# Six static tiles in a max-pool-and-subtract kernel, and subtracts without a wait for the slot's last stores

## The chip, the cores and the metric

The kernel runs on one core of one Trainium2 chip. The time is the device time of one execution in microseconds (us). It was 628.31 us, the median of 3 executions (628.23 to 628.38), before the change. "Span" is the time between the first and last thing in the profile; it is some 2 us shorter than the device time.

## The reference

```python
def reference(x):                                  # x: 8 x 64 x 256 x 256, float32
    x_r = x.reshape(B, C, oH, 8, oW, 8)
    pooled = x_r.max(axis=(3, 5))                  # maximum of each 8 x 8 window
    upsampled = np.repeat(np.repeat(pooled, 8, axis=2), 8, axis=3)
    return (x - upsampled).astype(np.float32)
```

134.2 MB come in and 134.2 MB go out. There is no matrix product.

## The kernel before

The work is cut into 32 tiles of 128 partitions. A full tile has 4 rows of 2048 numbers a partition: 32 KB a partition, 4096 KB in all. The loads are issued from SyncE's queue, the stores from ScalarE's; VectorE (DVE) takes the maximum of the windows in one reduce and subtracts row by row, in place. Tiles come from a pool of six that rotate: when tile i + 6 is asked for, the pool gives it the slot (the memory) of tile i and the framework adds what waits it thinks are needed. A wait goes by a semaphore, a counter that a transfer or an engine raises and that an instruction waits on.

```python
TILES = [([2, 2], [2, 2])] + [([4], [4])] * 30 + [([4], [2, 1, 1])]    # rows per load, rows per store
BUFS = 6
    data = ctx.enter_context(tc.tile_pool(name="data", bufs=BUFS))
    small = ctx.enter_context(tc.tile_pool(name="small", bufs=BUFS))

    def pool_and_subtract(dat, tops, R):
        # ... wins is dat by windows; one tensor_reduce (max) of R rows into tops
        for r in range(R):
            nc.vector.tensor_tensor(out=wins[:, r], in0=wins[:, r],
                in1=tops[:, r].unsqueeze(1).unsqueeze(3).to_broadcast([P, pH, oW, pW]),
                op=mybir.AluOpType.subtract)

    for loads, stores in TILES:
        dat = data.tile([P, size * ROW], F32, name="dat")
        pooled = small.tile([P, size * oW], F32, name="pooled")
        # ... cut: addresses
        for R in loads:
            nc.sync.dma_start(out=dat[:, part], in_=src[:, part])
        for R in stores:
            pool_and_subtract(dat[:, part], pooled[:, lo * oW : (lo + R) * oW], R)
            nc.scalar.dma_start(out=dst[:, part], in_=dat[:, part])
```

Of the kernel before, what the change touches and what calls it, by code (L numbers as in the profile page):

```python
# [1 line left out]

# [4 lines left out]

F32 = mybir.dt.float32
ROW = 2048

TILES = [([2, 2], [2, 2])] + [([4], [4])] * 30 + [([4], [2, 1, 1])]
BUFS = 6


@with_exitstack
def kernel(
    ctx: ExitStack,
    tc: tile.TileContext,
    x: bass.AP,
    out: bass.AP,  # L20
):
    nc = tc.nc
    P = nc.NUM_PARTITIONS
    B, C, H, W = x.shape
    pH = pW = 8
    oW = W // pW

    x_rows = x.rearrange("b c (oh ph) w -> (b c oh) (ph w)", ph=pH)
    out_rows = out.rearrange("b c (oh ph) w -> (b c oh) (ph w)", ph=pH)
    assert sum(sum(loads) for loads, _ in TILES) * P == x_rows.shape[0]  # L30
    size = max(sum(loads) for loads, _ in TILES)

    data = ctx.enter_context(tc.tile_pool(name="data", bufs=BUFS))
    small = ctx.enter_context(tc.tile_pool(name="small", bufs=BUFS))

    def pool_and_subtract(dat, tops, R):

        wins = dat.rearrange("p (r ph ow pw) -> p r ph ow pw", r=R, ph=pH, ow=oW)
        tops = tops.rearrange("p (r ow) -> p r ow", r=R)
        if R == 1:  # L40
            nc.vector.tensor_reduce(  # L41
                out=tops[:, 0],
                in_=wins[:, 0].rearrange("p ph ow pw -> p ow ph pw"),
                axis=mybir.AxisListType.XY,
                op=mybir.AluOpType.max,
            )
        else:
            nc.vector.tensor_reduce(  # L48
                out=tops,
                in_=wins.rearrange("p r ph ow pw -> p r ow ph pw"),  # L50
                axis=mybir.AxisListType.XY,
                op=mybir.AluOpType.max,
            )
        for r in range(R):
            nc.vector.tensor_tensor(  # L55
                out=wins[:, r],
                in0=wins[:, r],
                in1=tops[:, r].unsqueeze(1).unsqueeze(3).to_broadcast([P, pH, oW, pW]),
                op=mybir.AluOpType.subtract,
            )  # L60

    ctx.enter_context(tc.manual_schedule())
    at = 0
    for loads, stores in TILES:
        dat = data.tile([P, size * ROW], F32, name="dat")
        pooled = small.tile([P, size * oW], F32, name="pooled")

        rows = sum(loads)
        src = x_rows[at : at + P * rows].rearrange("(p r) d -> p (r d)", r=rows)
        dst = out_rows[at : at + P * rows].rearrange("(p r) d -> p (r d)", r=rows)  # L70
        at += P * rows
        lo = 0
        for R in loads:
            part = slice(lo * ROW, (lo + R) * ROW)
            nc.sync.dma_start(out=dat[:, part], in_=src[:, part])
            lo += R
        lo = 0
        for R in stores:
            part = slice(lo * ROW, (lo + R) * ROW)
            pool_and_subtract(dat[:, part], pooled[:, lo * oW : (lo + R) * oW], R)  # L80
            nc.scalar.dma_start(out=dst[:, part], in_=dat[:, part])
            lo += R


# [1 line left out]
_INS = ['x']  # L86
_OUTS = [((8, 64, 256, 256), 'float32')]


# [23 lines left out]
```

## Time and profile before

| | before |
|---|---|
| device time, median | 628.31 us |
| VectorE busy | 562.6 us, 90% of the span |
| VectorE idle, waiting for a load | 52.1 us |
| mean rate of the 16 DMA engines | 429 GB/s, 423 to 435 in the flat part |
| instructions in the profile | 364 |

The prediction below shows the lines behind this table. The busy engine is not the limit: VectorE waits for loads, while the DMA row shows its engines busy in every slice. This is the page's list of DMA queues (queue and kind: packets, MB, share of 16 engines), with the packet total ahead of it:

```profile
DMA packets 9794, 268.46 MB, mean 429 GB/s; under 512 B 1088, under 2 KB 1088, under 8 KB 1088
## 3 DMA queue, kind: packets, MB, share of 16 engines
q1 hardware_dynamic: 4752, 134.22, 49.9%
q10 hardware_dynamic: 5040, 134.22, 49.7%
q14 instruction: 2, 0.02, 0.0%
```

q1 and q10 are the loads and the stores. q14 carries instructions to the core (below, a fetch): two packets of 8192 bytes in the whole run, a share that prints as 0.0%.

### The profile page before, as it was taken

The numbers are of one execution on the slowest core, as the hardware profiler recorded it, in microseconds if no ns is written. First come the engines' busy times: TensorE is split into PE (matmuls) and PEld (weight loads), VectorE is DVE, ScalarE is ACT, GpSimd is POOL, SyncE is SP. The second block draws the span as 40 slices with busy tenths as digits, with TensorE's granted clock in tenths as the row PEclk, the third lists the DMA queues.
The fourth block names the chain that finished last, engine by engine and source line by source line (L and its number), as shares of the span: only waits on it lengthen the run. The fifth ranks groups of instructions, "written<-read, shape, count | busy, mean of one in ns | idle before, by whom it ended". The sixth has DMA issues, their size and how long they took to land.

```text
span 626.5 us, 364 instructions
## 1 busy us (share of the span) xinstructions
DVE 562.6 (90%) x163; POOL 0.2 (0%) x4
## 2 busy tenths in 40 slices
DVE  4999999988898888988889888899888898888983
POOL 0000000000000000000000000000000000000000
DMA  8999999999999999999999999999999999999997
GB/s 368 402 447 424 435 435 435 435 435 435 435 435 432 433 427 431 427 429 435 435 435 433 435 435 435 435 435 435 433 435 433 425 433 433 423 435 435 435 434 337
DMA packets 9794, 268.46 MB, mean 429 GB/s; under 512 B 1088, under 2 KB 1088, under 8 KB 1088
## 3 DMA queue, kind: packets, MB, share of 16 engines
q1 hardware_dynamic: 4752, 134.22, 49.9%
q10 hardware_dynamic: 5040, 134.22, 49.7%
q14 instruction: 2, 0.02, 0.0%
HBM read 134.22 MB, written 134.22 MB: 428 GB/s over the span
## 4 chain that ended last, share of the span: by engine, by line
DVE 90%; another core or an unknown queue 7%; DMA 1%; issue 0%
DVE dat L55 45%; DVE pooled L48 44%; DMA dat<-in_x_dram 1%; DVE pooled L41 1%
## 5 line engine op out<-in xcount | busy, mean ns | idle before, releaser
L48 DVE TENSOR_REDUCE pooled<-dat 128x128 f32<-128x8192 f32 (+1 forms) x33 | 273.8, 8297 | 52.1 <-DMA dat<-in_x_dram 52.1
L55 DVE TENSOR_TENSOR dat<-dat,pooled 128x2048 f32<-128x2048 f32 x128 | 285.0, 2287 | 1.2
L41 DVE TENSOR_REDUCE pooled<-dat 128x32 f32<-128x2048 f32 x2 | 4.6, 2278 | 0.0
L97 POOL MEMSET const-bfloat16-1.0<- 128x1 bf16 x1 | 0.1, 101 | 0.0
L97 POOL MEMSET const-uint8-127<- 128x1 uint8 x1 | 0.1, 101 | 0.0
L97 POOL MEMSET const-float32-0.0<- 128x1 f32 x1 | 0.1, 98 | 0.2 <-issue 0.2
L97 POOL MEMSET const-float32-1.0<- 128x1 f32 x1 | 0.1, 98 | 0.0
## 6 DMA issues: line engine op xcount, KB each, us to landing
dat<-in_x_dram SPq DMA_DIRECT2D x31, 4096.0 KB, 62.4
out_dram<-dat ACTq DMA_DIRECT2D x30, 4096.0 KB, 36.0
out_dram<-dat ACTq DMA_DIRECT2D x3, 2048.0 KB, 19.8
dat<-in_x_dram SPq DMA_DIRECT2D x2, 2048.0 KB, 9.5
out_dram<-dat ACTq DMA_DIRECT2D x2, 1024.0 KB, 10.4
```

What stands on the lines that cost most here:

```text
L41: nc.vector.tensor_reduce(out=tops[:, 0], in_=wins[:, 0].rearrange("p ph ow pw -> p ow ph pw"), axis=mybir.AxisListType.XY, op=mybir.AluOp ...
L48: nc.vector.tensor_reduce(out=tops, in_=wins.rearrange("p r ph ow pw -> p r ow ph pw"), axis=mybir.AxisListType.XY, op=mybir.AluOpType.max,)
L55: nc.vector.tensor_tensor(out=wins[:, r], in0=wins[:, r], in1=tops[:, r].unsqueeze(1).unsqueeze(3).to_broadcast([P, pH, oW, pW]), op=mybir ...
L97: nc = _bacc.Bacc("TRN2", target_bir_lowering=False, num_devices=1)
```

## The change

The intent: a subtract should not have to wait for the stores that last read its slot, because the load of the tile has already waited for them. Six tiles are allocated once and used in turn, and each subtract is declared independent of those stores.

```diff
-    data = ctx.enter_context(tc.tile_pool(name="data", bufs=BUFS))
-    small = ctx.enter_context(tc.tile_pool(name="small", bufs=BUFS))
+    data = ctx.enter_context(tc.tile_pool(name="data", bufs=1))
+    dats = [data.tile([P, size * ROW], F32, name=f"dat{i}") for i in range(BUFS)]
+    tops = [data.tile([P, size * oW], F32, name=f"tops{i}") for i in range(BUFS)]
...
-            nc.vector.tensor_tensor(
+            sub = nc.vector.tensor_tensor(
...
+            for store in landed:
+                tc.declare_no_dep(sub.ins, store.ins, reason="the load waited for it")
...
-    for loads, stores in TILES:
-        dat = data.tile([P, size * ROW], F32, name="dat")
-        pooled = small.tile([P, size * oW], F32, name="pooled")
+    slots = [[] for _ in range(BUFS)]
+    for i, (loads, stores) in enumerate(TILES):
+        dat, pooled = dats[i % BUFS], tops[i % BUFS]
...
+        landed, slots[i % BUFS] = slots[i % BUFS], []
         for R in stores:
...
-            nc.scalar.dma_start(out=dst[:, part], in_=dat[:, part])
+            slots[i % BUFS].append(nc.scalar.dma_start(out=dst[:, part], in_=dat[:, part]))
```

More of the change, by code (lines that the diff above doesn't have):

```diff
@@ L31, with pool_and_subtract @@
     size = max(sum(loads) for loads, _ in TILES)
-    data = ctx.enter_context(tc.tile_pool(name="data", bufs=BUFS))
-    small = ctx.enter_context(tc.tile_pool(name="small", bufs=BUFS))
-    def pool_and_subtract(dat, tops, R):
+    data = ctx.enter_context(tc.tile_pool(name="data", bufs=1))
+    dats = [data.tile([P, size * ROW], F32, name=f"dat{i}") for i in range(BUFS)]
+    tops = [data.tile([P, size * oW], F32, name=f"tops{i}") for i in range(BUFS)]
+    def pool_and_subtract(dat, tops, R, landed):
         wins = dat.rearrange("p (r ph ow pw) -> p r ph ow pw", r=R, ph=pH, ow=oW)
@@ L77 @@
         lo = 0
+        landed, slots[i % BUFS] = slots[i % BUFS], []
         for R in stores:
             part = slice(lo * ROW, (lo + R) * ROW)
-            pool_and_subtract(dat[:, part], pooled[:, lo * oW : (lo + R) * oW], R)
-            nc.scalar.dma_start(out=dst[:, part], in_=dat[:, part])
+            pool_and_subtract(dat[:, part], pooled[:, lo * oW : (lo + R) * oW], R, landed)
+            slots[i % BUFS].append(nc.scalar.dma_start(out=dst[:, part], in_=dat[:, part]))
             lo += R
```

## The prediction

> **What bounds the kernel now.** I read the page first for the share of each engine and the DMA rate, then the queue's waits, then the chain in time at a tile without the wait and at one with it, then the busy time by stretches.
>
> ```profile
> span 626.5 us, 364 instructions
> DVE 562.6 (90%) x163; POOL 0.2 (0%) x4
> ...
> DMA  8999999999999999999999999999999999999997
> GB/s 368 402 447 424 435 435 435 435 435 435 435 435 432 433 427 431 427 429 435 435 435 433 435 435 435 435 435 435 433 435 433 425 433 433 423 435 435 435 434 337
> ...
> HBM read 134.22 MB, written 134.22 MB: 428 GB/s over the span
> ...
> L48 DVE TENSOR_REDUCE pooled<-dat 128x128 f32<-128x8192 f32 (+1 forms) x33 | 273.8, 8297 | 52.1 <-DMA dat<-in_x_dram 52.1
> L55 DVE TENSOR_TENSOR dat<-dat,pooled 128x2048 f32<-128x2048 f32 x128 | 285.0, 2287 | 1.2
> ```
>
> The chain credits VectorE (DVE) with 90%, and that is a trap: DVE is busy 562.6 us but still sits idle for 52.1 us, all of it before a reduce and all of it until a load lands. The DMA row is at 9 in every slice but the first and the last, and from the fifth slice on the rate is flat at 423 to 435 GB/s. A flat rate that never dips, with the compute engine waiting for it, is a transfer limit. The subtracts (L55), which the change touches, have 1.2 us of idle before them in all, and no releaser.
>
> In the middle, two consecutive reduces start at 307.48 and 326.82 us, so a full tile takes 19.34 us. A tile moves 4096 KB in and 4096 KB out, 8.39 MB; over 19.34 us that is 434 GB/s. DVE needs 8.69 us (reduce) + 8.90 us (four subtracts) = 17.6 us of it and waits for the other 1.7 us. So DVE has 9% of slack, the DMA engines none.
>
> The waits of the load queue (what it waited for: us in total, times, longest):
>
> ```profile
> SPq L75 <- DMA out_dram<-dat: 500.5, 27, 19.0
> ...
> SPq L75 <- DMA dat<-in_x_dram: 21.4, 2, 16.5
> ```
>
> The first line is the true ordering of a slot: the load that refills a slot waits on the load queue until the store that last read the slot has landed. That wait stays in the changed kernel. The second shows that a load sometimes waits for an older load: in the trace's semaphores each transfer signals one of eight, taken in turn by loads and stores alike, and a transfer that reuses one waits for its previous user.
>
> Busy time by stretch (start to end, length, DVE busy, POOL busy, clock, DMA share, GB/s):
>
> ```profile
> 0.00:24.80 24.80, 16.71 (x6) 0.20 (x4) 1.00 0.94 377
> ...
> 200.00:598.00 398.00, 360.07 (x105) 0.00 (x0) 1.00 1.00 433
> 598.00:616.00 18.00, 17.78 (x7) 0.00 (x0) 1.00 0.98 423
> 616.00:626.50 10.50, 0.00 (x0) 0.00 (x0) 1.00 0.71 300
> ```
>
> Everything that is not DMA at full rate is at the two ends. At 433 GB/s the first 24.8 us would have moved their 24.8 x 377 GB/s in 21.6 us, so 3.2 us are lost there; the last 10.5 us lose 3.2 us in the same way. The change touches neither end: the first six tiles carry no store wait, and the last stretch has no DVE instruction.
>
> **What the Trainium skill says.** "DMA: Bandwidth & Descriptors", section "Where 436 GB/s comes from", puts the ceiling of the 16 ports at 435.2 GB/s. The trace agrees: the flat slices read 435. It also names about 358 GB/s as what binds traffic with HBM; this case's 428 over the span contradicts that for a core running alone, and the trace decides. "Perfetto Trace Analysis", section "Identifying Dependency Chains", says that an instruction that waits on several engines may get EventSemaphore instructions put before it. The trace shows just that: 26 such instructions of 21 ns on DVE's queue at the subtract's line, first at 113.2 us and last at 597.9 us, one for each of tiles 6 to 31. "VectorE: DVE Perf Modes", section "The DRAIN you can't avoid", reports that semaphores between DVE instructions added nothing to a chain of copies. For this kernel the next reading checks it.
>
> **The change, part by part.**
>
> Removed: the 26 waits of a subtract for a store. Each is a store that the tile's load has already waited for; the reduce waits for that load, the subtract for the reduce. So the semaphore is always satisfied when the wait is reached. What is left is the handling, at most 21 ns each: 26 x 21 ns = 0.55 us if all of it lay in DVE's path. Does it? The chain at tile 1, without such a wait, and at tile 30, with one:
>
> ```profile
> 25.82 8.61 DVE pooled L48
> 34.43 0.02 issue
> 34.45 8.90 DVE dat L55 x4
> ```
>
> ```profile
> 578.51 8.70 DVE pooled L48
> 587.21 0.02 issue
> 587.23 8.90 DVE dat L55 x4
> ```
>
> The step from the reduce to the first subtract is 0.02 us in both, and the four subtracts take 8.90 us in both. In the queue's own record the extra wait starts some 14 ns after its reduce has started (at tile 6, just before), so it is over while the 8.69 us reduce runs. It costs DVE 0 us, within the 10 ns that these views resolve. And even 0.02 us a tile would come out of the 1.7 us that DVE waits for the load anyway. On the path that sets the end: 0.
>
> Moved: the tiles. Six tiles of 32 KB a partition and six small ones of 512 bytes are the same memory as before, with the same rotation, and the refill still waits for the slot's stores. Reduces, subtracts, transfers, shapes and sizes stay: 35 reduces (273.8 + 4.6 us), 128 subtracts (285.0 us), 33 loads, 35 stores, 268.46 MB. Cost 0.
>
> Possibly moved: which of the eight semaphores a transfer takes, since slots are no longer released and allocated while the program is put in order. I can't see that order from the trace of before. The room for it is large: a load takes a median 62.4 us to land and a store 36.0, at one each per 19.34 us, so (62.4 + 36.0) / 19.34 = 5.1 transfers are in flight, fewer than eight. At the start, five loads (two of 2.1 MB and three of 4.2 MB, 16.8 MB) are queued at once, 16.8 / 433 = 39 us of work for the DMA, before any load that could have to wait for a semaphore is missed. I allow plus or minus 1 us.
>
> Sum: 628.3 - 0 (waits) + 0 (tiles) +- 1 = about 628.2 us.
>
> **The rivals.**
>
> The removed wait was real. If the wait held back the subtracts, they would start late, with a store named as releaser. Against it: 1.2 us of idle before all 128 of them, no releaser. It would be worth at most those 1.2 us, that is 627.1, and only if DVE set the end.
>
> DVE gets ahead and more transfers overlap. An earlier subtract issues its store earlier, which frees its slot earlier. Against it: the DMA engines are at share 1.00, so an earlier issue only lengthens the queue. The floor is 268.46 MB / 435.2 GB/s = 616.9 us for the bytes alone; the reported time is 1.9 us over the span (628.4 against 626.5). Over 2% faster means under 615.7, a span of 613.8 us and 437 GB/s from the first to the last microsecond, more than any long stretch reaches. Excluded as far as this trace goes.
>
> A new wait takes its place: a load also has to wait for a younger transfer because the semaphores fall differently, or the subtract waits for a still older store. An older store is landed by definition, cost 0. A misplaced load wait must leave the DMA engines idle to cost anything; before has stores held up in this way (at tile 8 the store's semaphore wait is recorded as 19.4 us) with the rate in that slice still 435. A bad rotation through the whole run could slow every tile. 2% is 12.6 us, or 0.4 us for each of 32 tiles, and would show as a dip in the GB/s row. Possible, unlikely; it would make some 635 to 645 us.
>
> **Range and chances.** Executions of before spread by 0.15 us. To that I add the 1 us for another semaphore order, and somewhat more for a different mix of loads and stores (the slices of before vary between 423 and 435 with that mix). So 626.2 to 630.0. Faster by over 2% needs more than the ports have given: 0.01. Slower by over 2% needs an idle DMA that I see no reason for: 0.02. Within 2%: 0.97.
>
> **What would show it right or wrong.** Right: no semaphore instruction at the subtracts' line on DVE's queue (26 before); the reduce-to-subtract step still 0.02 us; four subtracts still 8.90 us; idle before the reduces still some 50 us, for the load; the tile's period still 19.3 us; a flat GB/s row of 423 to 435; the load queue still waiting some 500 us for stores. Wrong: slices below 420 in the middle, DVE idle before reduces well over 60 us, or load-queue waits on loads in place of stores (the new wait); or the period under 19.2 us (the ports were not the limit).

## The result, and the profile after

The changed kernel took 627.71 us, the median of 6 executions (627.54 to 628.94), against 628.27 us for before (628.22 to 628.38). The ratio is 0.9994, 95% interval 0.9981 to 1.0007: the same within 2%, and by this interval alone not even clearly different. (A ratio is the mean time of one kernel's fast runs over that of the other's of the same rounds, so it is not quite the ratio of the medians.) Five of the six executions lie between 627.54 and 627.77; the sixth, 628.94, is the one whose profile follows.

The page of the kernel after:

```profile
span 627.0 us, 338 instructions
DVE 562.5 (90%) x163; POOL 0.2 (0%) x4
...
GB/s 368 407 439 425 435 435 435 435 435 435 433 435 435 433 435 426 431 431 431 431 435 433 431 435 435 431 435 435 435 435 435 433 433 433 431 433 431 433 433 328
DMA packets 9793, 268.45 MB, mean 428 GB/s; under 512 B 1088, under 2 KB 1088, under 8 KB 1088
...
q14 instruction: 1, 0.01, 0.0%
...
L53 DVE TENSOR_REDUCE tops<-dat 128x128 f32<-128x8192 f32 (+1 forms) x33 | 273.8, 8296 | 53.4 <-DMA dat<-in_x_dram 53.4
L60 DVE TENSOR_TENSOR dat<-dat,tops 128x2048 f32<-128x2048 f32 x128 | 284.9, 2285 | 1.2
```

The 26 semaphore instructions are gone (338 against 364 instructions): this line of before, from the view of its subtracts' line, has no counterpart after.

```profile
L55 DVEq EVENT_SEMAPHORE  x26: 21/21/21, 113.2 to 597.9; - x26
```

Nothing on VectorE moved: 273.8 us of reduces as before, 284.9 against 285.0 us of subtracts, 1.2 us of idle before the subtracts both times, 53.4 against 52.1 us of waiting for loads. The rate is as flat as before.

The chain at tile 30, in order of time:

```profile
579.77 8.70 DVE tops L53
588.47 0.02 issue
588.49 8.89 DVE dat L60 x4
```

The step from the reduce to the first subtract is still 0.02 us, with the wait gone. What the load queue waited for:

```profile
SPq L82 <- DMA out_dram<-dat: 501.3, 27, 19.4
...
SPq L82 <- DMA dat<-in_x_dram: 21.3, 2, 16.2
```

This is before again (500.5 and 21.4 us). The queue's own record shows each load and each store taking the same one of the eight semaphores as before, so the term that I left open, another order of semaphores, is zero.

So the profile says "nothing happened", and five executions of six say "0.6 us less". Besides the waits there are two candidates: there is one packet less on q14, and the static allocation may bring something of its own. The experiments had to find out whether 0.6 us is real, and if so whose it is.

### The profile page after: what moved, and what is told of

Read it like the earlier page. It is cut to its first block, busy times and chain, and to the rows that moved or that the text cites. A ratio compares the mean times of both kernels' runs of the same rounds, so it can differ in the third digit from the quotient of the medians.

```text
span 627.0 us, 338 instructions
## 1 busy us (share of the span) xinstructions
DVE 562.5 (90%) x163; POOL 0.2 (0%) x4
## 4 chain that ended last, share of the span: by engine, by line
DVE 90%; another core or an unknown queue 7%; DMA 1%; issue 0%
DVE dat L60 45%; DVE tops L53 44%; DMA dat<-in_x_dram 1%; DVE tops L46 1%
## 5 line engine op out<-in xcount | busy, mean ns | idle before, releaser
L53 DVE TENSOR_REDUCE tops<-dat 128x128 f32<-128x8192 f32 (+1 forms) x33 | 273.8, 8296 | 53.4 <-DMA dat<-in_x_dram 53.4
L60 DVE TENSOR_TENSOR dat<-dat,tops 128x2048 f32<-128x2048 f32 x128 | 284.9, 2285 | 1.2
L46 DVE TENSOR_REDUCE tops<-dat 128x32 f32<-128x2048 f32 x2 | 4.6, 2278 | 0.0
```

The costliest lines, as they stand in the source:

```text
L46: nc.vector.tensor_reduce(out=tops[:, 0], in_=wins[:, 0].rearrange("p ph ow pw -> p ow ph pw"), axis=mybir.AxisListType.XY, op=mybir.AluOp ...
L53: nc.vector.tensor_reduce(out=tops, in_=wins.rearrange("p r ph ow pw -> p r ow ph pw"), axis=mybir.AxisListType.XY, op=mybir.AluOpType.max,)
L60: sub = nc.vector.tensor_tensor(out=wins[:, r], in0=wins[:, r], in1=tops[:, r].unsqueeze(1).unsqueeze(3).to_broadcast([P, pH, oW, pW]), op ...
```

## The experiments

Twelve kernels ran, in three groups; the kernels of a group ran on one chip and share the runs of before. The diffs are cut to the lines that matter, some put more simply.

### Which part of the change, and is there a gain at all?

**static_one_wait**: the static tiles without the declaration.

```diff
-            for store in landed:
-                tc.declare_no_dep(sub.ins, store.ins, reason="the load waited for it")
```

> Six static tiles, no declared independence. In the built program only one of the 26 waits is left (tile 6, third subtract), so the allocation alone removes 25. My theory (DMA bound, the wait is free): 627.5 to 628.4 us, ratio to before 0.999 to 1.000, no wait at the subtracts but one. Rival A (the 0.6 us that the change seems to have won is real and comes from the removed waits): 627.7, as the changed kernel. Rival B (what was won comes from the declaration): 628.3.

**static_26_waits**: the static tiles, with the 26 waits of before put back.

```diff
-                tc.declare_no_dep(sub.ins, store.ins, reason="the load waited for it")
+                if r == 0:
+                    tc.add_manual_dep(sub.ins, store.ins.name, mybir.DependencyInfo(mybir.DependencyClass.Sync, ...), ...)
```

> Six static tiles, with a wait added to the first subtract of each of tiles 6 to 31 for the stores that last read its slot: the 26 waits of before on the allocation of after. My theory: the same time as the changed kernel of the same rounds, within 0.3 us. Rival A (the waits cost 26 x 21 ns = 0.55 us): 0.55 us slower than the changed kernel. Rival C (the allocation is worth the 0.6 us): as the changed kernel, and rotating_declared as before.

**rotating_declared**: the rotating pool of before, with the declaration.

```diff
+            for store in landed:
+                tc.declare_no_dep(sub.ins, store.ins, reason="the load waited for it")
```

> The rotating tiles of before, with the declaration of independence of after. The built program still has all 26 waits: they come from the release of a rotating tile and not from the memory that the subtract writes. So it is before again, a control for noise. My theory: 628.2 to 628.4, ratio 1.000. If it differs from before by over 0.3 us, then 0.6 us is noise.

**after_again**: the changed kernel once more, unedited.

> The changed kernel itself, on the chip of the three others. My theory: within 0.3 us of static_26_waits and static_one_wait; some executions near 628.9 as in the first measurement. If it is 0.5 to 0.6 us under before again, the small gain is real in some way, and the other three tell from which part it comes.

Measured, five timed executions each; before had 628.36 us (628.07 to 628.50) in these rounds:

| kernel | waits at subtracts | median us | lowest to highest | ratio to before, 95% interval |
|---|---|---|---|---|
| after_again | 0 | 627.59 | 627.52 to 627.81 | 0.9989, 0.9977 to 1.0002 |
| static_one_wait | 1 | 627.79 | 627.59 to 627.94 | 0.9991, 0.9978 to 1.0005 |
| rotating_declared | 26 | 628.36 | 628.23 to 628.95 | 1.0002, 0.9990 to 1.0015 |
| static_26_waits | 26 | 628.40 | 628.17 to 629.47 | 1.0005, 0.9992 to 1.0017 |

Each interval alone still holds 1, but the executions of these rounds fall into two groups that do not overlap: those of the kernels with no or one wait end at 627.94, those of the kernels with 26 begin at 628.07, before included. (The 628.94 of the first measurement would break this; I had expected some like it here, and none came.) The gain of 0.77 us (628.36 less 627.59) is there, and it goes with the waits and not with the allocation: static tiles with 26 waits are as slow as rotating ones. My theory, by which static_26_waits should have matched the changed kernel within 0.3 us, missed (0.81 us apart).

Two facts about the change come with this. The declaration does nothing on a rotating pool: all 26 waits stay; in the built program they come from the release of the tile. And on static tiles it removes a single wait; the allocation removes the other 25. The trace of static_one_wait shows where that one sits: it is carried by the third subtract of tile 6 itself, with no semaphore instruction, so this kernel has 338 instructions, as the changed one.

### Is it VectorE's time?

**two_subs_rotating** is before, and **two_subs_static** is after, both with every subtract done twice (a wrong result), so that VectorE sets the end.

```diff
-        for r in range(R):
+        for r in [*range(R), *range(R)]:
```

> Before, with every subtract done twice (a wrong result on purpose): VectorE then needs 8.7 + 8 x 2.2 = 26.3 us a tile against 19.3 of the DMA, so VectorE sets the end and its waits are exposed. 8.0 (first load) + 32 x 26.4 + 4.5 (last store) + 1.9 = some 859 us for both this and two_subs_static. My theory (the wait is over while the reduce runs): this minus two_subs_static is 0 within 0.1 us. Rival (the wait costs 21 ns of VectorE each and was only hidden by DMA): 0.55 us. Rival (the semaphore handling costs over 100 ns when exposed): over 2.6 us.

> After, with every subtract done twice (a wrong result on purpose). Some 859 us, equal to two_subs_rotating within 0.1 us by my theory; 0.55 us or over 2.6 us below it by the rivals.

They took 858.47 us (858.39 to 858.56) with the waits and 858.53 us (858.49 to 858.57) without: 0.06 us apart, the wrong way for the rival. VectorE is now the limit beyond doubt, as the page of two_subs_rotating shows; it waits for the first load and never again:

```profile
DVE 842.3 (98%) x291; POOL 0.2 (0%) x4
...
L48 DVE TENSOR_REDUCE pooled<-dat 128x128 f32<-128x8192 f32 (+1 forms) x33 | 273.5, 8289 | 8.0 <-DMA dat<-in_x_dram 8.0
```

So the rival "26 x 21 ns of VectorE" falls, although its number (0.55 us) lay close to the gain: with VectorE as the limit, 26 waits cost nothing measurable. One reservation: in the trace of two_subs_rotating the waits moved. They stand in front of a tile's sixth subtract and run 0.13 us into the fifth (2.28 us long), not beside the reduce. So this run shows that a wait beside a running VectorE instruction is free; that those of before, beside the reduce, are free as well rests on the unchanged 0.02 us step. The waits cost 0.77 us where VectorE has slack, and nothing where it has none. The cost has to sit elsewhere.

### What is the floor, and what do the kept waits cost?

**no_vector**: no VectorE instruction at all (a wrong result; the output is x).

```diff
-            pool_and_subtract(dat[:, part], pooled[:, lo * oW : (lo + R) * oW], R, landed)
```

> After without any VectorE instruction: each store waits for its load alone, the output is x (a wrong result on purpose). My theory (the DMA engines set the time): 624 to 628 us, within 1% of before, GB/s flat at 430 to 435. Rival (the chain load, reduce, subtract, store holds the transfers back): 617 us or less, the bytes at full rate.

It took 626.85 us (626.79 to 626.95), 0.9976 of before. Removing 562.6 us of busy time from the engine that the chain credits with 90% is worth 1.6 us (628.43 less 626.85). Its page, rate by slice, shows the same plateau with nothing else to do:

```profile
GB/s 346 436 426 436 436 436 436 436 428 434 428 430 434 430 436 436 436 436 436 428 434 426 432 434 430 436 436 436 436 436 430 430 428 432 434 430 436 436 436 369
```

It came inside the 624 to 628 us that I expected. The DMA engines set the time; that is now shown, not argued. And there is no q14 row at all on this page: zero packets of instructions.

**three_slots**: three static tiles in place of six.

```diff
-BUFS = 6
+BUFS = 3
```

> After with three slots in place of six. The load queue's 500 us of waits for stores are back-pressure by my theory. A slot needs a load at half rate (4.19 MB at 216 GB/s = 19.4 us), 17.6 us of VectorE and a store at half rate (19.4), 56.4 us[...]: 628 to 650 us. Rival (the wait for the store is itself the limit): slot time of now 6 x 19.34 = 116 us does not shrink, and the time about doubles.

It took 657.51 us (655.17 to 660.11), ratio 1.0465. The rival (about double) is far off; my own range ended at 650, so I missed too. The pages tell why: with the other transfers beside it a load took 22.5 us to land and a store 21.5, where I had put 19.4 for each. (An allowance without a run behind it is cut from the expectation above; the 56.4 us alone would be 18.8 us a tile.)

```profile
GB/s 385 401 337 450 418 450 383 420 448 420 386 436 416 434 403 410 381 428 351 436 412 410 428 408 428 405 414 436 416 422 424 407 405 408 444 418 418 418 418 321
...
dat<-in_x_dram SPq DMA_DIRECT2D x31, 4096.0 KB, 22.5
out_dram<-dat ACTq DMA_DIRECT2D x30, 4096.0 KB, 21.5
```

22.5 + 17.6 + 21.5 = 61.6 us for a slot, or 20.5 us a tile with three of them, over the 19.34 us of the DMA engines. This is what a kept wait looks like when it does cost: the rate swings between 337 and 450 GB/s from slice to slice. With six slots the rate stays flat, and I read the 500 us of waiting for stores as back-pressure: the queues are full, and the wait costs nothing.

### The instructions themselves

What 26 waits do bring with them is 26 instructions. The page counts one instruction packet less with them gone. I looked at what such a packet does to the data around it. Each transfer ends with 16 increments of its semaphore, and the trace has the time of every one; since some 16 data packets are under way at any time, I take each increment as one DMA engine's. For each transfer I took how far the last increment came behind the median of the 16. In static_26_waits, the trace in which it is plainest, this reads, in us (a selection of the stores; not a view of the profile tool):

```
stores landing at    171   190  | 211   230  ...   578   598  | 606   615   623   625
last of 16          0.18  0.17  | 1.03  0.97       0.90  0.90 | 1.67  1.65  1.61  1.60
last but one        0.17  0.16  | 0.17  0.15       0.54  0.56 | 0.55  0.58  0.58  0.59
instruction packet       at 195.9                        at 602.1
```

After each packet one engine, and only one, falls 0.8 to 0.9 us further behind, and it makes up little of that: 0.13 us in the next 120 us, then nothing for 270 us. Whatever it lags at the end is added to the run: the kernel ends when the last increment of the last store is in. The second packet lies just before the end, at 602.1 us; without the 26 instructions it is not needed before the end.

The packet records show where the time goes. An instruction packet takes 0.31 us. The 32 KB data packet that begins where it ends (within 5 ns, so I take it to be on the same engine) then takes 1.56 to 1.82 us, where the median data packet takes 1.21. In ten of the eleven traces of the table below (all but after, of which more at the end), from 25 us on, these are the only data packets out of some 7,700 a trace that take over 1.3 us: 18 of them, one behind each of the 18 instruction packets. So one fetch puts its engine 0.66 to 0.92 us back, 0.80 us on average.

With the waits alone this is a correlation. Four kernels were made to break it: they change the number of VectorE instructions against the number of waits.

**no_waits_plus_26**: no waits, 26 small instructions in their place.

```diff
+    bits = data.tile([P, 512], F32, name="bits")
...
+            if i >= 6 and lo == 0:
+                nc.vector.memset(bits[:, i : i + 1], 0.0)
```

> After (no wait at a subtract) with one small memset of 128x1 on VectorE in each of tiles 6 to 31, in place of the 26 waits: as many instructions on VectorE as before. New theory (a shorter instruction stream saves one 8 KB instruction fetch near the end, and each fetch puts one of the 16 DMA engines some 0.7 us behind): two fetches within the run, the second at some 602 us, last landing 1.3 to 1.7 us behind the median engine, 628.3 us as before. Rival (the wait itself costs the 0.7 us): 627.6 as after. Rival (VectorE's extra work costs): VectorE has 1.7 us of slack a tile, nothing.

**waits_minus_26**: all 26 waits, 26 subtracts fewer (a wrong result).

```diff
-        for r in range(R):
+        for r in range(2 if 10 <= i < 23 else R):      # i: the tile
```

> Before with its 26 waits, but the last two subtracts left out in 13 tiles (10 to 22), 26 instructions fewer on VectorE (a wrong result on purpose). New theory: one fetch within the run, last landing some 0.7 us behind, 627.6 us as after, although all waits are there. Rival (the wait costs): 628.4 as before.

**no_waits_plus_160** and **no_waits_plus_288**: five and nine small instructions in every tile.

```diff
+            if lo == 0:
+                for k in range(5):                     # 9 in the other
+                    nc.vector.memset(bits[:, 5 * i + k : 5 * i + k + 1], 0.0)
```

> After with five memsets of 128x1 a tile on VectorE, 160 in all: 128 instructions more than 32. New theory: one or two fetches more than after (two or three within the run), each worth some 0.7 us: 628.3 to 629.1. Rival (the wait costs, fetches nothing): 627.6. VectorE's own 5 x some 0.1 us a tile lies within its slack of 1.7 us.

> After with nine memsets of 128x1 a tile, 288 in all. New theory: three or four fetches within the run, one more than with 160, 629.0 to 629.9 if the lags add up on one engine; if they fall on different engines, no more than 628.3. VectorE's 9 x some 0.1 us a tile still lies within its slack of 1.7 us; if memsets cost over 0.2 us each, VectorE becomes the bound and the run says nothing.

The queue row of each page, in this order: no_waits_plus_26, waits_minus_26, no_waits_plus_160, no_waits_plus_288.

```profile
q14 instruction: 2, 0.02, 0.0%
```

```profile
q14 instruction: 1, 0.01, 0.0%
```

```profile
q14 instruction: 3, 0.02, 0.0%
```

```profile
q14 instruction: 4, 0.03, 0.0%
```

All kernels that are DMA bound with six slots, by instruction packets (before as in the last rounds; "lag" is the last increment of the last store behind the median one, in the profiled execution; after is the first measurement, whose profiled execution is the odd one of 628.94 us):

| kernel | waits | packets | median us | lag us |
|---|---|---|---|---|
| no_vector | 0 | 0 | 626.85 | 0.29 |
| after_again | 0 | 1 | 627.59 | 0.68 |
| after | 0 | 1 | 627.71 | 1.75 |
| static_one_wait | 1 | 1 | 627.79 | 0.89 |
| waits_minus_26 | 26 | 1 | 627.76 | 1.04 |
| before | 26 | 2 | 628.38 | 1.46 |
| rotating_declared | 26 | 2 | 628.36 | 1.45 |
| static_26_waits | 26 | 2 | 628.40 | 1.60 |
| no_waits_plus_26 | 0 | 2 | 628.44 | 1.47 |
| no_waits_plus_160 | 0 | 3 | 629.17 | 2.28 |
| no_waits_plus_288 | 0 | 4 | 629.98 | 3.08 |

The waits don't order this table, the packets do. With 26 waits and one packet the kernel is as fast as the changed one; with no wait and two packets it is as slow as before. From zero to four packets the time rises by 3.13 us, 0.78 us a packet, and the lag by 2.79. At the two ends of the table the interval of the ratio to before leaves out 1: 0.9963 to 0.9990 with no packet, 1.0014 to 1.0039 with four. The rival "the wait itself costs" is out by both of the crossed kernels. A cost of each instruction is out as well: from 338 to 364 instructions the time rises by 0.85 us, and from 364 to 498 by only 0.73 (after_again, no_waits_plus_26, no_waits_plus_160).

Two more readings of the traces say that it is one late engine and nothing else. In all of these kernels but after, the median increment of the last store came 623.5 to 623.9 us after the span's start, with VectorE's work or without; only the last increment moved, from 624.0 (no_vector) to 626.8 us (no_waits_plus_288). And where the DMA engines have slack, the lag goes away: two_subs_rotating has three packets, and its last store's last increment is 0.09 us behind the median.

The new theory had put 0.7 us on a packet, a little low: no_waits_plus_160 (629.17) and no_waits_plus_288 (629.98) came out 0.07 and 0.08 us above the ranges expected of them. In no_waits_plus_26 the second packet came at 571.8 us, not at the 602 I expected; the time was right all the same.

VectorE's extra work isn't what costs. In no_waits_plus_288 the 288 memsets (59 ns each in its groups) come out of the time in which VectorE waits for full-tile loads:

```profile
L55 DVE TENSOR_REDUCE tops<-dat 128x128 f32<-128x8192 f32 x30 | 260.6, 8685 | 39.7 <-DMA dat<-in_x_dram 39.7
L55 DVE TENSOR_REDUCE tops<-dat 128x64 f32<-128x4096 f32 x3 | 13.3, 4419 | 10.6 <-DMA dat<-in_x_dram 10.6
L93 DVE MEMSET bits<- 128x1 f32 x288 | 5.6, 59 | 0.1
```

Some 40 us of slack are left. The DMA rate of that kernel sits at 426 to 434 GB/s on the plateau; nobody would find the 1.6 us in that row.

No kernel with the right result beat the changed one. Fewer VectorE instructions still (no packet at all, perhaps 626.9 us as an estimate from the table) would need another way to write the subtracts and was not tried.

## Why the prediction was right or wrong

**The time and the class.** 628.2 us with a range of 626.2 to 630.0 was predicted, 627.71 measured, in a class of "same" that had 0.97. Right.

**What bounds the kernel.** Right, and now shown: without VectorE the time is 626.85 us.

**"It costs DVE 0 us."** Right: same 0.02 us step after the reduce, and 858.47 against 858.53 us where VectorE is the limit. This also answers what the prediction left to be checked of "VectorE: DVE Perf Modes" in the Trainium skill, section "The DRAIN you can't avoid": there a semaphore after each of eight copies added nothing. The waits here are for stores, not between VectorE instructions, and they added nothing either.

**"On the path that sets the end: 0."** Wrong by a small amount, and this is the step that failed. The removed waits were priced by what they do (wait, 21 ns) and where (beside the reduce), and the path was taken to be "DMA engines moving 268.46 MB". The waits are also 26 instructions, these have to be fetched, and the fetch goes through the same DMA engines that set the end. The missing term is one packet of 8192 bytes: -0.77 us between before and after_again of the same rounds (-0.56 in the first measurement). It would have been found by asking of the page's 0.0% row: who pays for these two packets? Bytes are the wrong measure: 8192 bytes at 435 GB/s over 16 engines are 0.02 us, but they fall on one engine and hold up the data packet behind them, 0.80 us in all, and in these traces that engine gains little of it back.

**"Moved: the tiles. Cost 0."** Right: 628.40 us for static tiles with the waits of before, 628.36 for the rotating ones.

**"Which of the eight semaphores", +-1 us.** The term was zero: the order came out the same. The allowance covered the missed term by luck, so the class and the range say little about the mechanism.

**The rivals.** "The removed wait was real" was given at most 1.2 us and 627.1 us of time; its size was near, its mechanism is refuted. "DVE gets ahead": no_vector is as far ahead as any kernel can get, and ends 1.58 us earlier than before, which two fetches at 0.78 us account for. "New wait" did not come. The signs named for "right" all came (26 semaphore instructions gone, steps of 0.02 and 8.89 us, 53.4 us of idle, a period of 19.36 us, a flat rate, 501.3 us of waiting for stores), but they are signs of VectorE, of waits and of mean rates, and none of them shows the missed term.

**What stays open.** Why the data packet behind a fetch takes 0.35 to 0.61 us longer than the others: no run shows it. Which of the 16 engines it is: the records carry no engine number; that lags add up (0.68, 1.46, 2.28, 3.08) says that it is mostly the same one. The execution of the changed kernel at 628.94 us has one packet, but its last increment lags by 1.75 us: engines fell behind again near 230, 250 and 328 us with no instruction packet there, and 24 data packets of 1.31 to 1.65 us stand at 227, 243 to 246, 320 to 324 and 556 to 595 us. A second engine drifts back slowly in most runs (0.17 to 0.56 us between 330 and 600 us in static_26_waits). And the first fetch comes at 164 to 166 us in the kernels without the 26 waits whose subtracts are as before, at 196 us in those with them. None of these is explained.

## What to carry to other kernels

Waits that were always satisfied cost their engine nothing here (858.47 us with 26 of them, 858.53 without), so removing them was worth nothing on that engine, although the profile counted 26 of them. Where the DMA engines have no slack, though, each DMA engine is its own path: what landed on one of them alone (here 8 KB of instructions per some 127 instructions on VectorE) delayed the end by nearly its full cost, and the mean rate did not show it. It is a small cost: 0.8 us of 628. Read the small rows of the queue list, and compare the last of a transfer's 16 increments with the rest.

## What the Trainium skill lacked or had wrong

- "Runtime: NRT & Kernel Launch", section "Instruction fetch mechanics", calls the cost of crossing a block of instructions "mostly hidden". In this DMA-bound kernel it was not: 0.78 us for each fetch (626.85 us with none, 629.98 us with four). It doesn't say that a fetch competes with data on one DMA engine.
- The same section gives blocks of 16 KiB, 256 instructions. The runs show packets of 8192 bytes; in no_waits_plus_288 they came at 73.7, 242.5, 417.6 and 592.8 us. The last two are 175.2 us apart, that is 9.06 tiles of 19.34 us with 14 VectorE instructions each, one packet per 127 instructions.
- No page that I read says that an engine which falls behind in a saturated stream stays behind, so that a delay of one of 16 engines is added to the end: in static_26_waits the last increment went from 0.17 to 1.03 us behind after one fetch and was still 0.90 us behind 390 us later.
- "DMA: Bandwidth & Descriptors", section "Where 436 GB/s comes from", says without a condition that for transfers between HBM and SBUF the lower figure of some 358 GB/s binds. With one core running, no_vector held 426 to 436 GB/s in every slice but the first and the last. The page's own table, under "Measured", has 425 GB/s for one core alone; it is that sentence which lacks the condition.
